# Four engines put in program order through branch A of a hybrid encoder block

## The chip, the cores and the metric

One core of one Trainium2 chip runs the whole block. The metric is the device time of one execution in microseconds. The engines are TensorE (PE, its weight loads PEld), VectorE (DVE), ScalarE (ACT), GpSimd (POOL) and SyncE (SP), which here issues nearly all DMAs.

## The reference, cut to what matters

1024 tokens and 16 meta tokens (1040 keys), width 1024. Branch A is differential attention with four heads: each has two attention maps, which are subtracted before they meet the values.

```python
s1 = einsum('bqhd,bkhd->bhqk', q1, k1) * scale - slope * dist
s2 = einsum('bqhd,bkhd->bhqk', q2, k2) * scale - slope * dist
attn = softmax(s1) - lam * softmax(s2)
y = rms_norm(einsum('bhqk,bkhe->bqhe', attn, v), subln_g) * (1 - lambda_init)
...
merged = sigmoid(ga) * (y_a @ w_ba) + sigmoid(gb) * (y_b @ w_bb)
```

The gates `ga` and `gb` are two projections of the normed input, 1024 columns each. A windowed attention (branch B) comes before the stretch that the change touches; the output projection and a SwiGLU feed-forward come after it.

## The kernel before

All matmuls keep float32 precision by splitting each operand into a high part (a copy that rounds, on ScalarE) and a low part (a subtraction, on GpSimd or VectorE), and adding three products.

**The loop over tiles.** The 32 tiles of branch A are four heads of eight query blocks (`n = 8 h + t`). A tile's work is written as generators, and the string `SLOTS = "sgsgsngsgsstntnt"` says in which order their steps are taken. TensorE runs in that order (`tc.manual_schedule`); where no such order is given, a planner that simulates the program orders an engine's instructions.

- `s`, six steps (`scores_a`): three chunks of 392, 392 and 256 keys for map 1, then three for map 0. TensorE makes the scores in a bank tagged `sc` (five of them); VectorE adds the distance and keeps a running minimum (line 817), writing to SBUF. With the minimum of the third chunk ScalarE takes the exponential of all 1040 columns and their sum (824); then VectorE takes the reciprocal (826), and for map 1 GpSimd scales by it and by minus lambda (828). At the end VectorE joins the maps: map 0 times its reciprocal plus map 1 (837) and a copy of the last 16 columns (838).
- `t`, three steps (`transpose_a`), for the tile before: TensorE transposes four, four and one blocks of 128 keys (849); ScalarE writes the high part (852), VectorE the low part (853).
- `n`, three steps of the tail: after every second tile the values (862), in three parts; after every fourth their norm: square and scaled copy on ScalarE (869, 871), sums on TensorE, a factor on VectorE and GpSimd (877, 878), the product on VectorE (884), a store.
- `g`, four steps (six in tile 1): one quarter each of a gate's matmuls (751), twelve of 512 columns a gate. Four steps go ahead of head 0 and ten ahead of each other head. So head 0 has 38 steps and a head of eight tiles 42: head 1 starts in the middle of gate 9, head 2 with gate 20, head 3 in the middle of gate 30. After the ten steps a gate starts at a tile's first `g` in heads 1 and 3, and at its third in head 2, as in head 0 from tile 2 on.

**The gates.** 50 partial products (`order_g`), seven for each of eight blocks but those made earlier. Gates 0 to 17 have kinds 2, 5 and 3; from gate 18 on two each of 1, 6, 7 and 4 take turns. For each, a raw weight is loaded (624; five buffers, asked for four gates ahead) and split into `gop` (117 and 118, four buffers, three gates ahead). A result of kind 1, 6 or 7 is added by VectorE to a sum kept from earlier (756), which is loaded from DRAM into one of three buffers `gk` when the weight is split (636); other results are copied by ScalarE (759, two buffers). Then it is stored (760). Two consecutive products use one bank of TensorE's results after another, two banks in all.

**Head changes.** At the top of a head's first tile the loads of its queries, keys and values are asked for (671 to 688). Their tiles have one buffer each, so a load waits for its last reader in the head before.

**Held back.** In tile 0 alone ScalarE and VectorE run in program order; there the splits are put into a list `held_back`, and `let_go` takes them out one at a time.

Of the kernel before, what the change touches and what calls it, by code (L numbers as in the profile page):

```python
# [19 lines left out]
P = 128  # L20
# [7 lines left out]
AH = 4  # L28
# [8 lines left out]
N_WAIT = 3  # L37
PP2 = 2
# [35 lines left out]
def encoder_block(ctx: ExitStack, tc: tile.TileContext, x, meta, norm_mix, w_in, lq1, lk1, lq2, lk2,  # L74
# [553 lines left out]
    def g_split(n, op=None):  # L628
        p, k = order_g[n]
        if op is None:  # L630
            op = gpool.tile([P, 2, 4, P], F32R, tag="gop", name=f"gop{p}_{k}", bufs=GO_BUFS)
        split(op[:, 0], op[:, 1], g_raw.pop((p, k)), nc.gpsimd)
        g_ready[p, k] = op
        if p in (1, 6, 7):
            kept = g_kept[p, k] = gpool.tile([P, 512], F32, tag="gk", name=f"gk{p}_{k}", bufs=GK_BUFS)
            nc.sync.dma_start(kept, g_place(p, k))
# [38 lines left out]
    def load_a0(h, q, k):  # L675
        q[0] = apool.tile([P, S], F32R, tag="q0", name=f"aq{h}_0")
        nc.sync.dma_start(f32(q[0]), qa_d[h][0])
        if h:
            load_k(h, 0, k[0])
            return q, k, load_v(h)  # L680
        return q, k
# [59 lines left out]

    def gate_steps():
        for n, (p, k) in enumerate(order_g):
            g_ahead(n + 1)
            op, act = g_ready.pop((p, k)), G_ACT[p]
            if p in (2, 5, 1):
                g_bank[k] = pp_bank(f"pg{p}_{k}")
            ps = g_bank[k]
            for c in range(4):
                for i, (a, b) in enumerate(((0, 0), (0, 1), (1, 0))):  # L750
                    nc.tensor.matmul(ps, op[:, a, c], quad(b, *act)[:, c], start=(p in (2, 5, 1) and c == 0 and i == 0),  # L751
                                     stop=(p in (2, 3, 4) and c == 3 and i == 2), skip_group_check=True)
                if c == 3:
                    if p in (1, 6, 7):
                        st = g_kept.pop((p, k))
                        nc.vector.tensor_tensor(st, ps, st, ALU.add)  # L756
                    else:
                        st = gpool.tile([P, 512], F32, tag="g", name="gate_stage", bufs=G_BUFS)
                        nc.scalar.copy(st, ps)
                    nc.sync.dma_start(g_place(p, k), st)  # L760
                    if (p, k) in ((5, 3), (5, 7), (3, 7)):
                        later_p = {(5, 3): 6, (5, 7): 7, (3, 7): 4}[p, k]
                        load_sums(later_p, *G_ACT[later_p])
                yield
# [9 lines left out]
    ld = *ld, load_v(0)  # L774
# [24 lines left out]
    behind_first, n_tile = [], [0]  # L799

    def scores_a(h, t, ld, s):
        slope = 2.0 ** -(2 * (h + 1))
        qs, ks, _ = ld
# [3 lines left out]
        u0 = 896 - t * P  # L807
        for m in (1, 0):
            s[m] = s0s[t % 2] if m == 0 else apool2.tile([P, L], F32, tag="s1", name=f"as1_{nm}", bufs=S_BUFS[1])
            low = far_a  # L810
            for i, (k0, n) in enumerate(A_CHUNKS):
# [8 lines left out]
                if i == 1 and behind_first:  # L820
                    behind_first.pop(0)()
                if i < 2:
                    yield
            nc.scalar.activation(s[m][:, 0:L], s[m][:, 0:L], AF.Exp, bias=low, scale=-1.0, accum_out=dn[:, m:m + 1])  # L824
            def scaled(m=m):
                nc.vector.reciprocal(dn[:, m:m + 1], dn[:, m:m + 1])  # L826
                if m:
                    (nc.gpsimd if t % 4 in COMBINE_POOL else nc.vector).tensor_scalar(  # L828
                        s[1][:, 0:L], s[1][:, 0:L], dn[:, 1:2], neglam, ALU.mult, ALU.mult)
            if m and n_tile[0] == 0:  # L830
                behind_first.append(scaled)
            else:
                scaled()
            if n_tile[0] == 0:
                let_go(1)
            yield
        nc.vector.scalar_tensor_tensor(s[0][:, 0:L], s[0][:, 0:L], dn[:, 0:1], s[1][:, 0:L], ALU.mult, ALU.add)
# [28 lines left out]
    def normed_a(h, c, py):  # L866
# [3 lines left out]
        yg = apool2.tile([P, 512], F32, tag="yg", name=f"yg_{nm}", bufs=2)  # L870
# [27 lines left out]
    def turn(done):  # L898
        h, t, s, at_, v = done
        yield from transpose_a(h, t, s[0], at_)  # L900

    def later(done):
        h, t, s, at_, v = done
        if t % 4 == 1:
            acc[0] = bank(psum2, "acc", f"apy_{h}_{t}", 1)
        yield from values_a(h, t, v, at_, acc[0])
# [10 lines left out]

    for n in range(AH * NT + T_LAG):
        n_tile[0] = n
        if n == 0:  # L920
            order_first = tc.manual_schedule(engines={mybir.EngineType.Activation, mybir.EngineType.DVE})
            order_first.__enter__()
        scoring, turning = iter(()), iter(())
        if n < AH * NT:
            h, t = divmod(n, NT)
            if t == 0:
                if h:
                    ld = load_a0(h, *load_a1(h))
# [3 lines left out]
            s = [None, None]  # L932
            tiles.append((h, t, s, at_, ld[2]))
# [5 lines left out]
        if n >= T_LAG:  # L939
            turning = turn(tiles[n - T_LAG])  # L940
        for what in SLOTS if n != 1 else "sgsgsngsgssggtntnt":
            if what == "s":
                next(scoring, None)
            elif what == "t":
                next(turning, None)
            elif what == "n":
                step_tail()
            else:
                fill(1)
        for _ in scoring:  # L950
            pass
        if n == 0:
            let_go(9)
            held_back = None
            order_first.__exit__(None, None, None)
# [3 lines left out]
        for _ in turning:  # L959
            pass  # L960
# [586 lines left out]
```

## Time and profile before

| | us |
|---|---|
| median of three runs | 1442.53 (1442.18 to 1443.05) |
| the profiled execution | 1443.88 |
| its span, first to last instruction | 1442.1 |
| granted TensorE clock | 0.998 |

A timeline line gives the start in us from the start of the span, the duration (of several merged instructions from the first's start to the last's end), engine, line, operation, what it writes from what it reads, shapes, the count, and in brackets the idle time before it with what ended it. A waits line reads: who, for whom, us in total, times, longest. A windows line gives the stretch, its length, the busy time and count of PE, PEld, DVE, ACT and POOL, the granted clock, the DMA engines' share and GB/s. In the chain of waits a piece has its start and its length. A DMA line ends with the size and the median time to landing. L817 is line 817.

### The profile page before, as it was taken

What the parts mean: (1) busy time and instruction counts of PE and PEld (TensorE: products, weight loads), DVE (VectorE), ACT (ScalarE), POOL (GpSimd) and SP (SyncE); (2) the same over time, 40 slices, a digit from 0 to 9 for tenths busy, and PEclk for the clock granted to TensorE, in tenths of its full rate; (3) what the DMA queues carried; (4) which work ended last, traced back from release to release, by engine and by line L of the source; (5) the groups of instructions that cost most, each with busy time, mean ns of one, the idle gap of its engine ahead of it and who ended that gap; (6) DMA issues with size and microseconds to landing.
All of it is one profiled execution on the core that took longest, in us unless ns stands there. A gap on an engine that the chain in (4) does not pass through costs nothing.

```text
span 1442.1 us, 21169 instructions
## 1 busy us (share of the span) xinstructions
PE 1421.4 (99%) x7279; PEld 1219.8 (85%) x7279; DVE 898.4 (62%) x1624; ACT 679.3 (47%) x1290; POOL 644.5 (45%) x605
## 2 busy tenths in 40 slices
PE   8999999999999999999999999999999999999997
PEld 6988989988889989888888788888888888788886
DVE  7468536637787979625514966555555554787567
ACT  6366535546565655545314643333333333444444
POOL 5589227744333433425522775544454442000444
PEclk9999999999999999999999999999999999999999
DMA  8367668996558464586602534333333333964443
GB/s 245 87 211 231 196 160 273 278 286 230 176 177 271 133 220 148 183 258 209 212 22 102 154 99 164 101 105 103 110 100 103 98 109 101 327 207 142 124 129 139
DMA packets 188891, 242.41 MB, mean 168 GB/s; under 512 B 18208, under 2 KB 115936, under 8 KB 188784
## 3 DMA queue, kind: packets, MB, share of 16 engines
q1 hardware_dynamic: 188784, 241.07, 52.9%
q8 instruction: 57, 0.93, 0.3%
q14 instruction: 50, 0.41, 0.1%
HBM read 157.45 MB, written 77.00 MB: 163 GB/s over the span
## 4 chain that ended last, share of the span: by engine, by line
PE 82%; POOL 6%; issue 4%; DVE 4%; DMA 3%; ACT 1%; SPq 0%; POOLq 0%; ACTq 0%; DVEq 0%
PE pg L1328 28%; PE pg L751 8%; PE pd L1422 8%; PE po L1105 6%; PE ppa L796 6%; PE aps L814 4%; PE apy L862 3%; PE pp_qb L214 3%; POOL oa L118 3%; PE pp_ka L214 2%; PE pp_va L214 2%; PE apt L849 2%; PE pp_qa L214 2%; PE bpt L356 1%; PE bpy L362 1%
## 5 line engine op out<-in xcount | busy, mean ns | idle before, releaser
L118 POOL TENSOR_TENSOR wop<-wf,wop 128x512 fp32r<-128x512 f32 x128 | 171.8, 1347 | 166.4 <-ACT wop L117 150.5
L1328 PE MATMUL pg<-t,wop 128*128 128x512 f32 x1056 | 242.6, 389 | 0.0
L1328 PEld LDWEIGHTS pg<-t,wop 128*128 128x128 f32 x1056 | 198.3, 188 | 41.1
L1422 PE MATMUL pd<-ob,oa 128*128 128x512 f32 x924 | 210.7, 390 | 0.8 <-POOL oa L118 0.4
L1422 PEld LDWEIGHTS pd<-ob,oa 128*128 128x128 f32 x924 | 173.2, 188 | 38.2 <-DVE ob L118 1.1
L1328 PE MATMUL pg<-b,wop 128*128 128x512 f32 x792 | 185.6, 392 | 2.4 <-DVE c L1337 2.4
L1328 PEld LDWEIGHTS pg<-b,wop 128*128 128x128 f32 x792 | 149.5, 189 | 34.2 <-issue 2.4
L751 PE MATMUL pg<-hT_hi,gop 128*128 128x512 f32 x384 | 142.3, 395 | 0.0
L118 POOL TENSOR_TENSOR oa<-ra,oa 128x512 fp32r<-128x512 f32 x33 | 44.0, 1336 | 171.2 <-ACT oa L117 169.8
L117 ACT ACTIVATE wop<-wf 128x512 fp32r<-128x512 f32 x128 | 80.2, 631 | 83.2 <-PE pg L1328 48.6
L118 POOL TENSOR_TENSOR gop<-gr,gop 128x512 fp32r<-128x512 f32 x47 | 66.0, 1406 | 106.3 <-ACT gop L117 106.3
L117 ACT ACTIVATE oa<-ra 128x512 fp32r<-128x512 f32 x77 | 48.7, 632 | 106.1 <-PE pd L1422 45.3
L824 ACT ACTIVATE as<-as,amn 128x1040 f32<-128x1040 f32 x64 | 74.5, 1164 | 45.4 <-DVE amn L817 34.4
L1163 DVE TENSOR_TENSOR s<-wf,wf 128x512 f32<-128x512 f32 x22 | 25.5, 1160 | 105.6 <-DMA wf<-in_w_ff_gate_dram 57.7
L814 PE MATMUL aps<-ak,aq 128*128 128x392 f32 (+1 forms) x384 | 89.3, 327 | 1.6 <-DVE amn L817 1.1
L1105 PE MATMUL po<-woh,mT 128*128 128x512 f32 x384 | 88.0, 390 | 0.0
L1105 PEld LDWEIGHTS po<-woh,mT 128*128 128x128 f32 x384 | 71.9, 188 | 14.8
L751 PEld LDWEIGHTS pg<-hT_hi,gop 128*128 128x128 f32 x384 | 72.2, 188 | 11.2 <-DVE gk L756 0.2
L814 PEld LDWEIGHTS aps<-ak,aq 128*128 128x128 f32 x384 | 69.3, 188 | 14.6 <-DVE amn L817 2.0
L343 POOL TENSOR_SCALAR bs<-bs,bdn 128x432 f32<-128x432 f32 (+1 forms) x64 | 41.4, 665 | 85.9 <-DVE bdn L341 74.1
L751 PE MATMUL pg<-hT_lo,gop 128*128 128x512 f32 x192 | 75.8, 395 | 0.0
L828 POOL TENSOR_SCALAR as<-as,adn,neglam 128x1040 f32<-128x1040 f32 x32 | 38.9, 1216 | 57.5 <-DVE adn L826 43.9
(289 smaller groups left out, 3099.4 us busy)
## 6 DMA issues: line engine op xcount, KB each, us to landing
ra<-aop SPq DMA_DIRECT2D x77, 256.0 KB, 2.7
wf<-in_w_ff_gate_dram SPq DMA_DIRECT2D x24, 512.0 KB, 3.9
wf<-in_w_ff_up_dram SPq DMA_DIRECT2D x24, 512.0 KB, 3.9
aop<-as SPq DMA_DIRECT2D x44, 256.0 KB, 2.1
w_c<-in_w_in_dram SPq DMA_DIRECT2D x17, 512.0 KB, 6.1
aop<-c SPq DMA_DIRECT2D x33, 256.0 KB, 2.0
ts_d<-to SPq DMA_DIRECT2D x16, 512.0 KB, 3.8
gw<-in_w_in_dram SPq DMA_DIRECT2D x32, 256.0 KB, 4.1
```

Source lines behind the costliest of these rows:

```text
L117: nc.scalar.activation(hi, src, AF.Copy)
L118: lo_eng.tensor_tensor(lo, src, f32(hi), ALU.subtract)
L214: nc.tensor.matmul(ps[:, :n], a[:, c, :], b[:, c, at:at + n], start=(c == 0 and i == 0), stop=(c == DC - 1 and i == 2))
L343: nc.gpsimd.tensor_scalar(st[:, r, :W], st[:, r, :W], dn[:, r:r + 1], 1.0, ALU.mult, ALU.mult)
L751: nc.tensor.matmul(ps, op[:, a, c], quad(b, *act)[:, c], start=(p in (2, 5, 1) and c == 0 and i == 0), stop=(p in (2, 3, 4) and c == 3 and ...
L796: nc.tensor.matmul(ps, w[:, a, j, :], src(j, b, tk), start=(j == 0 and n == 0), stop=(j == 3 and n == 2))
L814: nc.tensor.matmul(ps[:, :n], qs[m][:, t * P:(t + 1) * P], ks[m][:, vv, k0:k0 + n], start=(vv == 0), stop=(vv == 1))
L824: nc.scalar.activation(s[m][:, 0:L], s[m][:, 0:L], AF.Exp, bias=low, scale=-1.0, accum_out=dn[:, m:m + 1])
L862: nc.tensor.matmul(py[:, cols], v[:kp, a, k, :], at_[:kp, k, b, :], start=(k == 0 and j == 0), stop=(k == 8))
L1105: nc.tensor.matmul(ps, mT[:, c, a, t * P:(t + 1) * P], wos[q, c][:, b], start=(c == 0 and n == 0), stop=(c == DC - 1 and n == 2))
L1328: nc.tensor.matmul(ps, op[:, x, c, :], b[:, y, c, :], start=(p in (1, 2, 5) and c == 0 and n == 0), stop=(p in (4, 2, 3) and c == 3 and n ...
L1422: nc.tensor.matmul(ps[u], oa[:, a, u * P:(u + 1) * P], ob[:, b, :], start=(p in (1, 2, 5) and j == 0 and k == 0), stop=(p in (2, 3, 4) and ...
```

## The change

- A manual order for ScalarE, VectorE, GpSimd and SyncE (`order_av`) spans the whole loop of branch A; before, ScalarE's and VectorE's covered tile 0 alone.
- `scores_a` only makes scores. The exponential (`exp_a`), the scaling of map 1 (`scale_a`) and the join (`join_a`) are called from the loop: exponential 1 after the third `s`, scaling after the fifth, exponential 0 after the first `t` (`EXP_AT`), the join of the tile before after the first `s` (`JOIN_AT`).
- A gate's result is written down one step later (`owed`, `gate_result`), behind the next gate's first quarter. With it goes the load of token sums into `hT`.
- Splits are held back through the whole loop; one is let go behind exponential 1 and one at the third `t`, or where a gate needs it at once.
- The load of a kept sum is put in a list with the split, and asked for after the second quarter of a gate, if fewer than three are held.
- The next head's loads are called in the last tile of a head: map 1's after the third `s`, map 0's after the sixth. Its values are loaded at tile 2.
- The scaled values `yg` have one buffer instead of two.

```diff
         if p in (1, 6, 7):
-            kept = g_kept[p, k] = gpool.tile([P, 512], F32, tag="gk", name=f"gk{p}_{k}", bufs=GK_BUFS)
-            nc.sync.dma_start(kept, g_place(p, k))
+            kept_to_do.append((p, k))
+
+    def load_kept():
+        p, k = kept_to_do.pop(0)
+        kept = g_kept[p, k] = gpool.tile([P, 512], F32, tag="gk", name=f"gk{p}_{k}", bufs=GK_BUFS)
+        nc.sync.dma_start(kept, g_place(p, k))
...
+    def gate_result(p, k, ps):
+        if p in (1, 6, 7):
+            while (p, k) not in g_kept:
+                load_kept()
+            st = g_kept.pop((p, k))
+            nc.vector.tensor_tensor(st, ps, st, ALU.add)
+        else:
+            st = gpool.tile([P, 512], F32, tag="g", name="gate_stage", bufs=G_BUFS)
+            nc.scalar.copy(st, ps)
+        nc.sync.dma_start(g_place(p, k), st)
...
     def gate_steps():
         for n, (p, k) in enumerate(order_g):
             g_ahead(n + 1)
+            while (p, k) not in g_ready:
+                let_go(1)
...
+                while owed:
+                    gate_result(*owed.pop(0))
+                if c == 1:
+                    while kept_to_do and len(g_kept) < GK_BUFS:
+                        load_kept()
                 if c == 3:
...
+                    owed.append((p, k, ps))
+                    if n == len(order_g) - 1:
+                        gate_result(*owed.pop(0))
...
+    def exp_a(s, m):
+        dn = s["of"]
+        nc.scalar.activation(s[m][:, 0:L], s[m][:, 0:L], AF.Exp, bias=s["low", m], scale=-1.0, accum_out=dn[:, m:m + 1])
+
+    def scale_a(t, s):
+        dn = s["of"]
+        nc.vector.reciprocal(dn[:, 1:2], dn[:, 1:2])
+        (nc.gpsimd if t % 4 in COMBINE_POOL else nc.vector).tensor_scalar(
+            s[1][:, 0:L], s[1][:, 0:L], dn[:, 1:2], neglam, ALU.mult, ALU.mult)
+
+    def join_a(s):
+        dn = s["of"]
+        nc.vector.reciprocal(dn[:, 0:1], dn[:, 0:1])
         nc.vector.scalar_tensor_tensor(s[0][:, 0:L], s[0][:, 0:L], dn[:, 0:1], s[1][:, 0:L], ALU.mult, ALU.add)
...
+    order_av = tc.manual_schedule(engines={mybir.EngineType.Activation, mybir.EngineType.DVE, mybir.EngineType.Pool, mybir.EngineType.SP})
+    order_av.__enter__()
     for n in range(AH * NT + T_LAG):
...
+        if n < AH * NT and t == 2 and h:
+            vs[h] = load_v(h)
+        scored = turned = 0
+        if n == AH * NT:
+            join_a(tiles[n - 1][2])
         for what in SLOTS if n != 1 else "sgsgsngsgssggtntnt":
...
+            if what == "s" and n < AH * NT:
+                next(scoring)
+                scored += 1
+                if scored == JOIN_AT and n:
+                    join_a(tiles[n - 1][2])
+                if scored == 3:
+                    exp_a(s, 1)
+                    if t == NT - 1 and h < AH - 1:
+                        ahead = load_a1(h + 1)
+                    let_go(1)
+                if scored == 5:
+                    scale_a(t, s)
+                if scored == 6 and n == 0:
+                    exp_a(s, 0)
+                if scored == 6 and t == NT - 1 and h < AH - 1:
+                    ahead = load_a0(h + 1, *ahead)
+            elif what == "t" and n:
+                next(turning)
+                turned += 1
+                if turned == EXP_AT and n < AH * NT:
+                    exp_a(s, 0)
+                if turned == 3:
+                    let_go(1)
...
+    order_av.__exit__(None, None, None)
     n_gates[0] += HOLD
     raw_w = []
     while tail:
         step_tail()
+        let_go(9)
         fill(3)
```

More of the change, by code (lines that the diff above doesn't have):

```diff
@@ L819, in scores_a @@
                 low = mn[:, m, i:i + 1]
-                if i == 1 and behind_first:
-                    behind_first.pop(0)()
                 if i < 2:
                     yield
[L824 to L835, printed above, removed]
-            yield
+            s["low", m] = low
+            yield
+    def exp_a(s, m):
[9 more added lines that the diff above has]
+        nc.vector.reciprocal(dn[:, 0:1], dn[:, 0:1])
         nc.vector.scalar_tensor_tensor(s[0][:, 0:L], s[0][:, 0:L], dn[:, 0:1], s[1][:, 0:L], ALU.mult, ALU.add)
@@ L927, in encoder_block @@
                 if h:
[L928 removed]
+                    ld = ahead
                 fill(G_HEAD if h else G_FIRST)
```

54 lines of the change are left out of this document (17 added, 37 removed).

## The prediction, made before the changed kernel was run

> **What bounds the kernel now.** I read the page's busy times first, then the busy time of the stretch that holds branch A's attention loop, then who waits there.
>
> ```profile
> PE 1421.4 (99%) x7279; PEld 1219.8 (85%) x7279; DVE 898.4 (62%) x1624; ACT 679.3 (47%) x1290; POOL 644.5 (45%) x605
> ...
> 325.00:605.00 280.00, 276.67 (x1699) 250.16 (x1697) 224.08 (x647) 167.55 (x316) 110.81 (x88) 1.00 0.59 193
> ...
> PE apt L849 <- DVE as L837: 1.1, 2, 1.0
> PE aps L814 <- DVE amn L817: 1.1, 3, 0.4
> PE aps L814 <- DMA ak<-ka_d: 0.5, 1, 0.5
> ```
>
> In these 280 us TensorE is busy 276.67 and idle 3.3; VectorE is busy 224, 80%. So TensorE bounds the loop, and all that a better order of the other engines can give back there is a few us: 1.1 waiting for the softmax difference, 1.1 for a score bank, 0.5 for a key load. What VectorE itself waits for costs TensorE almost nothing today.
>
> The tile is the unit to count in. The first score matmuls of five successive tiles (head 3, tiles 2 to 6) in the timeline:
>
> ```profile
> 542.51 0.60 PE L814 MATMUL aps<-ak,aq 128*128 128x392 f32 x2
> ...
> 549.07 0.63 PE L814 MATMUL aps<-ak,aq 128*128 128x392 f32 x2
> ...
> 556.26 0.61 PE L814 MATMUL aps<-ak,aq 128*128 128x392 f32 x2
> ...
> 563.83 0.60 PE L814 MATMUL aps<-ak,aq 128*128 128x392 f32 x2
> ...
> 572.48 0.60 PE L814 MATMUL aps<-ak,aq 128*128 128x392 f32 x2
> ```
>
> Tiles 2, 3, 4 and 5 take 6.56, 7.19, 7.57 and 8.65 us, 29.97 for a cycle of four, 7.49 a tile. TensorE's order is not changed. So what decides is whether the other engines, in the order now written down, can still do a tile in 7.49 us.
>
> **The written order, followed round once.** ScalarE and VectorE each run their list in order, so one late entry holds all behind it. From the new loop, tile n: the third score chunk of map 1, then its exponential (exp 1) on ScalarE; at the first transpose step ScalarE's high part of transpose block 0 of tile n-1, and only then exp 0 of tile n; at the next step block 1's high part on ScalarE and its low part on VectorE; then block 2. VectorE's next entry is the first score chunk of tile n+1, then the join of tile n (reciprocal, sum of the two maps, copy of 32 columns), then chunks 2 and 3, and then exp 1 of tile n+1. That closes a loop through both engines: exp 1, high 0, exp 0, high 1, low 1, low 2, chunk 1, reciprocal, sum, copy, chunk 2, chunk 3, exp 1. No link can be passed on its engine. Prices, from starts of instructions that follow each other without a gap in the timeline of VectorE and that of ScalarE:
>
> ```profile
> 544.20 0.61 DVE L817 CUSTOM_DVE_ANT_0 as<-aps,dist,far_a 128x392 f32<-128x392 f32 x1
> 544.75 0.68 DVE L853 TENSOR_TENSOR at<-apt,at 128x512 fp32r<-128x512 f32 x1
> 545.35 0.17 DVE L838 COPY as<-as 128x32 f32<-128x32 f32 x1
> 545.43 0.27 DVE L853 TENSOR_TENSOR at<-apt,at 16x128 fp32r<-16x128 f32 x1
> 545.63 0.60 DVE L817 CUSTOM_DVE_ANT_0 as<-aps,dist,amn 128x392 f32<-128x392 f32 x1
> ...
> 546.74 0.48 DVE L817 CUSTOM_DVE_ANT_0 as<-aps,dist_m,amn 128x256 f32<-128x256 f32 x1
> 547.15 0.69 DVE L756 TENSOR_TENSOR gk<-pg,gk 128x512 f32<-128x512 f32 x1
> 547.75 0.62 DVE L817 CUSTOM_DVE_ANT_0 as<-aps,dist,amn 128x392 f32<-128x392 f32 x1
> ...
> 550.38 0.16 DVE L826 RECIPROCAL adn<-adn 128x1 f32<-128x1 f32 x1
> 550.64 1.30 DVE L837 SCALAR_TENSOR_TENSOR as<-as,adn,as 128x1040 f32<-128x1040 f32 x1
> 551.86 0.62 DVE L817 CUSTOM_DVE_ANT_0 as<-aps,dist,amn 128x392 f32<-128x392 f32 x1
> ```
>
> ```profile
> 542.85 0.59 ACT L869 ACTIVATE ysq<-apy 128x512 f32<-128x512 f32 x1
> 543.33 0.69 ACT L871 ACTIVATE yg<-apy,gsub 128x512 f32<-128x512 f32 x1
> 543.90 0.28 ACT L852 ACTIVATE at<-apt 128x128 fp32r<-128x128 f32 x1
> ...
> 546.94 0.63 ACT L117 ACTIVATE gop<-gr 128x512 fp32r<-128x512 f32 x1 [2.76 <-issue]
> 547.48 1.15 ACT L824 ACTIVATE as<-as,amn 128x1040 f32<-128x1040 f32 x1
> 548.62 0.58 ACT L852 ACTIVATE at<-apt 128x512 fp32r<-128x512 f32 x1
> 549.10 1.16 ACT L824 ACTIVATE as<-as,amn 128x1040 f32<-128x1040 f32 x1
> 550.25 0.75 ACT L852 ACTIVATE at<-apt 128x512 fp32r<-128x512 f32 x2
> ```
>
> ScalarE: exp 1.14 (547.48 to 548.62), high 0 0.48, exp 0 1.15, high 1 0.58 until its result is there: 3.35. VectorE: low 1 0.60, low 2 0.20, chunk 1 0.55, reciprocal 0.26, sum 1.22, copy 0.08, chunk 2 0.55, chunk 3 0.48: 3.94. **The bare loop is 7.29 us.** Before, the same timeline shows the reciprocal and the sum starting at 550.38, while exp 0 (549.10) has only just ended, and blocks 1 and 2 after them: low 1, low 2 and chunk 1 were not between exp 0 and the sum. That is 1.35 us, and its loss is the heart of the change.
>
> On the loop come, by head:
> - the split of a gate weight, let go right behind exp 1: its copy stands between exp 1 and high 0, 0.54 (546.94 to 547.48). In heads 1 and 3, where a gate starts at a tile's first gate step, this is every tile; in heads 0 and 2 a gate starts at the third step, behind the place where splits are let go, and the split falls to the last transpose step, off the loop.
> - the gate result. In heads 1 and 3 it is written behind the join: its ScalarE copy is off the loop, its addition on VectorE is on it, 0.60 (547.15 to 547.75). In heads 0 and 2 it is written behind exp 1: the ScalarE copy is on the loop, 0.48, taken from the row below; an addition makes exp 0 wait for the last chunk of map 0: 0.60 + 0.55 + 0.55 + 0.16 + 0.48 = 2.34 on VectorE against 1.62 on ScalarE, so 0.72.
> - the square and the scaled copy of four tiles' values, once in four tiles, in the step behind exp 1: 0.48 + 0.57 = 1.05.
>
> Cycles of four: head 0 (copies) 4 x 7.77 + 1.05 = 32.1. Head 1 (splits) 4 x 7.83 + 1.05 = 32.4. Head 2 (three additions in four, one copy: 0.66 on average) 4 x 7.95 + 1.05 = 32.9. Head 3 (splits, additions three times in four) 4 x 8.28 + 1.05 = 34.2. Against 29.97 that is 2.1, 2.4, 2.9 and 4.2 a cycle; two cycles a head: **23.2 us.** This takes it that TensorE's long tile (8.65) lets the loop catch up what the short one (6.56) lost. Where it can't, each tile costs the longer of the two: in head 1 8.65 + 8.88 + 7.83 + 7.83 = 33.2, 3.2 a cycle, and likewise 3.0, 3.6 and 4.6 in heads 0, 2 and 3: 28.8 in all. From below: at a head's start TensorE has ten gate steps alone, and what lag is left then is hidden.
>
> ```profile
> 451.43 6.95 PE pg L751 x30
> ...
> 472.10 1.07 PE apy L862 x9
> ```
>
> (The second line, nine value matmuls, is for the next part.) Of the 6.95 us at most the lead that the five score banks allow is used: five chunks of at most 0.60 by the rows above and a gate step of 6.95 / 10 = 0.7 between them, 3.7 us a head: 23.2 - 14.8 = 8. I take 23, the sum itself: the lag cannot grow beyond the banks, so it is nearly as long in a head's second tile as in its last, and what a fill hides at its end is built up anew.
>
> **The splits held back all through.** At the start of gate n the split of gate n+3 is only queued; two places a tile let one go. The ten steps at a head's start queue two or three and let none go. In heads 1 and 3 they are let go in time. Head 2 begins with gate 20, so gate 23 starts at the third gate step of its first tile, one step behind the place that lets its split go. VectorE starts on that tile's chunk 1 0.4 us in, and ends chunk 3 0.55 + 0.26 + 1.22 + 0.08 + 0.55 + 0.48 = 3.1 later; then exp 1, the copy, and GpSimd:
>
> ```profile
> 547.65 1.28 POOL L118 TENSOR_TENSOR gop<-gr,gop 128x512 fp32r<-128x512 f32 x1 [4.32 <-ACT gop L117]
> ```
>
> High part ready at 0.4 + 3.1 + 1.14 + 0.63 = 5.3, low part at 6.6. TensorE is there after three chunks (at most 0.6 each), two steps of 0.7 and nine value matmuls (1.07): 4.3 or sooner; its third matmul, which takes the low part, 0.46 later. It waits 1.0 or more, then some 0.9: I take 2.5 us, once (0 if VectorE is far ahead, 3.3 if the chunks take half).
>
> **SyncE in order.** The load of a kept gate sum goes into one of three buffers, the next of which is just being stored; everything behind it on SyncE's queue stands. Behind it in a head's last tile stand the next head's eight query and key loads.
>
> ```profile
> SPq L636 <- DMA g_d<-gk: 30.0, 19, 3.9
> ...
> 446.43 0.33 SPq L671 DMA_DIRECT2D aq<-qa_d  x1
> ...
> 450.98 0.46 SPq L666 DMA_DIRECT2D ak<-ka_d  x1
> ...
> ak<-ka_d SPq DMA_DIRECT2D x12, 260.0 KB, 8.0
> ```
>
> Before, a kept load waited up to 3.9. For head 2 the loads went out from 446.43 to 450.98, so the last landed about 459.0; its first scores start after the fill, at 458.4, and map 0 is wanted some 4 us later. A delay of 3.9 makes map 0 late by about 0.5. Heads 2 and 3 can be hit. At head 1 the stores of gate results queue behind the head's loads:
>
> ```profile
> 395.16 0.59 ACT L759 COPY gate_stage<-pg 128x512 f32<-128x512 f32 x1 [5.21 <-DMA g_d<-gate_stage]
> 395.64 1.17 ACT L824 ACTIVATE as<-as,amn 128x1040 f32<-128x1040 f32 x1
> ```
>
> ScalarE stood 5.21 there and an exponential behind it. The new order keeps both buffers and the same neighbours, so it stays and may reach the next tile. I put +3 for the three head starts: from -2 (the value load, 1 MB, moved out of their way to tile 2, where values are first used late in tile 3) to +4 at each, +12. The store asked for one step later, the second buffer less for the scaled values (next used four tiles on) and the earlier order of loads cost nothing beside that. The waits of before that were quoted, 2.7, may go: -1 (0 to -3.3).
>
> **Sum.** 23 + 2.5 + 3 - 1 = +27.5. The profiled execution took 1443.88 us with a span of 1442.1, 1.3 above the median of 1442.53; the same addition to the median gives **1470**.
>
> [...] Sums and copies of VectorE are sometimes stretched:
>
> ```profile
> 514.42 1.30 POOL L118 TENSOR_TENSOR gop<-gr,gop 128x512 fp32r<-128x512 f32 x1 [0.74 <-ACT gop L117]
> ...
> 514.59 2.24 DVE L837 SCALAR_TENSOR_TENSOR as<-as,adn,as 128x1040 f32<-128x1040 f32 x1
> ```
>
> The sum took 2.24 instead of 1.30, and started 0.17 into a subtraction of GpSimd that ended 1.13 later: 1.13 + 1.22 = 2.35, so it waited it out. [...]
>
> **Rivals.**
> - *GpSimd under the join.* In heads 0 and 2 the split let go at the last transpose step puts GpSimd's 1.28 us where the join begins, on the loop: behind exp 0 come high 1, high 2 and the copy, 0.48 + 0.28 + 0.63 = 1.4, so GpSimd works from 1.4 to 2.7, and the sum is due at 0.58 + 0.60 + 0.20 + 0.55 + 0.26 = 2.2. That is 0.5 a tile, 0.94 at worst (2.24 less 1.30), over 16 tiles: +8 to +15, 1478 to 1485. Against: a weight that is late shifts GpSimd past the sum.
> - *SyncE decides.* +12 instead of +3 at the head starts and gate weights late behind them: 1480 to 1486. Against: weights are asked for four gates ahead.
> - *The lag is carried.* TensorE's lead and the fills take half of it or more: +8 to +19, 1450 to 1462.
> - *Faster.* The loop stays under 7.49, because the splits and gate results that stand on it fall into time in which ScalarE or VectorE would wait for the other anyway; then TensorE keeps its pace, the join comes always in time, and the 3.3 us of idle time in the stretch go: 1439. It decides at 29.97 a cycle, which the bare loop (4 x 7.29 + 1.05 = 30.2) only just misses. Against: the entries named stand between two links of the same engine, where there is no such time.
> - *Nothing:* the planner's order was already this one, and the time stays at 1442.5. Against: the rows from 549 to 552 stand in another order.
>
> **How the numbers follow.** Forecast 0.60 (its own range 1462 to 1480), carried lag 0.13, GpSimd 0.09, SyncE 0.05, faster 0.09, nothing 0.04. The range goes from the bottom of the carried lag, 1450, to near the top, 1484; faster, nothing and a part of the top, under 0.2, are left out. About 0.2% (2.9 us) is what can be told from no change. Slower 0.60 + 0.13 + 0.09 + 0.05 = 0.87, same 0.04, faster 0.09.
>
> **What would show it.** In the changed profile: tiles 2 and 3 of a cycle near 8 to 9 us instead of 6.56 and 7.19; ScalarE idle 3 to 4 us a tile before exp 1, put down to the third chunk's minimum; VectorE in the order low 1, low 2, chunk 1, sum; TensorE waiting before transposes for the sum and before score chunks for a bank; about 2.5 us before gate 23. After 620 us nothing but a shift. It is wrong if tiles keep their 6.56, or if TensorE's waits are for loads and not for VectorE.

## The result, and the profile after

The changed kernel took 1495.32 us (median of four runs, 1493.36 to 1499.97) beside 1442.79 for the kernel before: a ratio of 1.037, with an interval of 1.034 to 1.039. That is 52.5 us slower. The forecast was 27.5 slower, with 41.5 as the top of its range. Direction and place were right, the size was not.

The first part of the page after, then the stretches of the four heads (a windows view), then TensorE's waits from 320 to 660 us. The changed kernel has other line numbers: 836 makes the scores, 839 is VectorE's chunk, 849 the exponential, 860 the sum of the maps, 872 the transposes, 875 and 876 the high and low parts, 892 and 894 the square and the scaled copy, 898 the sums of squares, 119 and 120 the split of a weight, 776 the gate's matmuls, 756 and 759 their results.

```profile
PE 1446.1 (97%) x7279; PEld 1236.6 (83%) x7279; DVE 906.0 (61%) x1624; ACT 674.1 (45%) x1290; POOL 638.7 (43%) x605
```

```profile
326.00:401.00 75.00, 67.71 (x366) 58.38 (x365) 51.22 (x148) 39.32 (x76) 24.93 (x20) 0.95 0.43 134
401.00:483.00 82.00, 73.61 (x419) 65.23 (x418) 56.67 (x160) 39.91 (x78) 24.68 (x21) 0.94 0.57 184
483.00:566.00 83.00, 72.92 (x417) 64.87 (x416) 59.13 (x164) 38.07 (x73) 26.02 (x22) 0.94 0.49 158
566.00:640.00 74.00, 66.80 (x389) 60.92 (x388) 55.83 (x159) 35.70 (x69) 22.96 (x20) 0.91 0.38 125
```

```profile
PE apst L898 <- ACT ysq L892: 15.3, 7, 2.3
PE apt L872 <- DVE amn L839: 9.5, 12, 1.3
PE pg L776 <- ACT gop L119: 2.7, 2, 2.4
PE pg L776 <- POOL gop L120: 1.6, 3, 0.6
PE aps L836 <- DVE amn L839: 1.3, 3, 0.5
PE aps L836 <- DMA ak<-ka_d: 1.2, 1, 1.2
```

No engine has more instructions than before. TensorE, idle for 3.3 of 280 us in the loop before, now stands 33 us in these 314 (314 less the four busy times, 281.0), and its granted clock is 0.91 to 0.95 where it was 1.00. The longest wait is not one that the prediction priced for TensorE: the sums of squares (`apst`) wait seven times for ScalarE's square, 2.2 us each on average (1.81 to 2.33). Next come the transposes that wait for the softmax; loads are 1.2.

What the other engines wait for turned as foreseen. ScalarE before its exponentials and VectorE before its low parts, from the groups of the page after, and the same two groups of the loop before:

```profile
L849 ACT ACTIVATE as<-as,amn 128x1040 f32<-128x1040 f32 x64 | 74.5, 1164 | 133.4 <-DVE amn L839 133.3
...
L876 DVE TENSOR_TENSOR at<-apt,at 128x512 fp32r<-128x512 f32 (+1 forms) x96 | 50.1, 550 | 49.0 <-ACT at L875 48.9
```

```profile
L824 ACT ACTIVATE as<-as,amn 128x1040 f32<-128x1040 f32 x64 | 74.5, 1164 | 45.4 <-DVE amn L817 34.4 <-DVE as L838 8.9 <-POOL gop L118 1.4
```

```profile
L853 DVE TENSOR_TENSOR at<-apt,at 128x512 fp32r<-128x512 f32 (+1 forms) x96 | 50.8, 547 | 7.9 <-ACT at L852 7.7
```

ScalarE's idle time before an exponential that the minimum ends went from 34.4 to 133.3 us, and VectorE's for ScalarE's high part from 7.7 to 48.9. Each of the two stands for the other, while neither has more to do: that is the loop.

The tiles of head 3 after, by their first score matmuls, to be laid beside 6.56, 7.19, 7.57 and 8.65:

```profile
582.67 0.60 PE L836 MATMUL aps<-ak,aq 128*128 128x392 f32 x2
...
594.07 1.00 PE L836 MATMUL aps<-ak,aq 128*128 128x392 f32 x2
...
602.80 0.61 PE L836 MATMUL aps<-ak,aq 128*128 128x392 f32 x2
...
610.37 0.60 PE L836 MATMUL aps<-ak,aq 128*128 128x392 f32 x2
...
619.86 0.60 PE L836 MATMUL aps<-ak,aq 128*128 128x392 f32 x2
```

Tiles 2 to 5 take 11.40, 8.73, 7.57 and 9.49. The same reading of every tile, summed by place over the heads, with the loss against the same tiles before:

| tiles | before (heads 0, 1, 2, 3) | after | loss |
|---|---|---|---|
| 0 and 1 of heads 1 to 3 | 18.05, 16.09, 16.13 | 20.42, 21.03, 16.13 | +7.3 |
| 2 | 6.19, 6.53, 6.51, 6.56 | 8.93, 10.52, 11.62, 11.40 | +16.7 |
| 3, 4 and 5 | 23.98, 23.65, 23.36, 23.42 | 26.92, 24.25, 25.00, 25.79 | +7.6 |
| 6 | 6.51, 6.53, 6.78, 6.53 | 10.47, 10.74, 10.72, 11.72 | +17.3 |
| 7 of heads 0 to 2 | 14.69, 14.40, 15.42 | 16.45, 16.24, 15.15 | +3.3 |

These are 52.2; the last tile and its tail add 1.8, and everything after the loop is 2.4 shorter. Two thirds (34.0) lie in tiles 2 and 6, and seven of those eight are the tiles in which the square of four tiles' values stands. The eighth, tile 2 of head 0, has no values before it and takes 8.93.

**What a tile with a square looks like.** The timelines of TensorE, ScalarE and VectorE in head 1:

```profile
426.65 0.66 PE L872 MATMUL apt<-ident,as 128*128 128x128 f32 x4 [0.44 <-DVE amn L839]
429.64 1.34 PE L898 MATMUL apst<-ones,ysq 128*128 128x1 f32 x8 [2.33 <-ACT ysq L892]
430.84 1.31 PE L872 MATMUL apt<-ident,as 128*128 128x128 f32 x5
431.80 1.00 PE L836 MATMUL aps<-ak,aq 128*128 128x392 f32 x2
```

```profile
427.33 1.16 ACT L849 ACTIVATE as<-as,amn 128x1040 f32<-128x1040 f32 x1 [3.49 <-DVE amn L839]
...
428.49 0.61 ACT L119 ACTIVATE gop<-gr 128x512 fp32r<-128x512 f32 x1
429.01 0.58 ACT L892 ACTIVATE ysq<-apy 128x512 f32<-128x512 f32 x1
429.49 0.68 ACT L894 ACTIVATE yg<-apy,gsub 128x512 f32<-128x512 f32 x1
430.06 0.59 ACT L875 ACTIVATE at<-apt 128x512 fp32r<-128x512 f32 x1
430.53 1.18 ACT L849 ACTIVATE as<-as,amn 128x1040 f32<-128x1040 f32 x1
...
431.97 0.77 ACT L875 ACTIVATE at<-apt 128x512 fp32r<-128x512 f32 x2 [0.17 <-PE apt L872]
...
436.99 1.16 ACT L849 ACTIVATE as<-as,amn 128x1040 f32<-128x1040 f32 x1 [3.77 <-DVE amn L839]
```

```profile
432.60 0.88 DVE L876 TENSOR_TENSOR at<-apt,at 128x512 fp32r<-128x512 f32 x2 [1.16 <-ACT at L875]
433.41 0.60 DVE L839 CUSTOM_DVE_ANT_0 as<-aps,dist,far_a 128x392 f32<-128x392 f32 x1
...
434.20 1.30 DVE L860 SCALAR_TENSOR_TENSOR as<-as,adn,as 128x1040 f32<-128x1040 f32 x1
...
435.63 0.62 DVE L839 CUSTOM_DVE_ANT_0 as<-aps,dist,amn 128x392 f32<-128x392 f32 x1
...
436.40 0.48 DVE L839 CUSTOM_DVE_ANT_0 as<-aps,dist_m,amn 128x256 f32<-128x256 f32 x1
```

Exp 1, split, square, scaled copy, high 0, exp 0, high 1 and 2, low parts, chunk 1, sum, chunk 2, chunk 3: the predicted loop, once round from 427.33 to 436.99. TensorE has done its first four transposes and comes to the sums of squares; the square stands behind exp 1 and the split, so TensorE stops for 2.33 us in the middle of a tile. Its last five transposes stand behind those sums and are done at 432.15, so ScalarE's next copy (0.17) and VectorE's low parts behind it (1.16) wait as well. In such a tile the loop runs through TensorE too.

**What a tile without one looks like.** The next exponentials of map 1, in tiles 4 and 5 of head 1:

```profile
445.30 1.17 ACT L849 ACTIVATE as<-as,amn 128x1040 f32<-128x1040 f32 x1 [3.78 <-DVE amn L839]
...
453.60 1.17 ACT L849 ACTIVATE as<-as,amn 128x1040 f32<-128x1040 f32 x1 [3.77 <-DVE amn L839]
```

From 436.99 to 445.30 and from there to 453.60 the loop goes round in 8.31 us, and to the next, at 461.91, in 8.31 again, while TensorE's own lengths of these tiles were 7.43, 7.58 and 8.64 before. The loop runs at a pace of its own. Such plain rounds take, from tile 3 on, 8.50 in head 0, 8.31 in head 1, 8.53 to 8.89 in head 2 and 8.91 in head 3.

The same trace's granted clock, the third number from the end of a windows row: two 3.4 us stretches that hold such a stop, and in a second answer of the same view what followed each.

```profile
426.80:430.20 3.40, 1.07 (x9) 0.83 (x9) 2.23 (x9) 2.87 (x6) 0.96 (x1) 1.00 0.71 225
461.00:464.40 3.40, 0.84 (x6) 0.60 (x6) 2.46 (x11) 2.49 (x5) 0.64 (x1) 1.00 1.01 326
```

```profile
430.20:433.60 3.40, 3.40 (x15) 3.21 (x15) 1.76 (x5) 2.84 (x6) 2.51 (x3) 0.51 0.02 7
464.40:471.20 6.80, 6.80 (x25) 6.22 (x25) 4.33 (x10) 2.73 (x6) 2.84 (x3) 0.50 0.50 190
```

TensorE was busy for 1.07 and 0.84 of 3.40 us, and was then granted half its clock for 3.4 and 6.8 us. The trace has seven such pairs in the loop, one for each wait for a square, 41 us at half clock in all; before, the loop had none.

### The profile page after: what moved, and what is told of

Read it like the earlier page. It is cut to its first block, busy times and chain, and to the rows that moved or that the text cites. A ratio compares the mean times of both kernels' runs of the same rounds, so it can differ in the third digit from the quotient of the medians.

```text
span 1494.1 us, 21147 instructions
## 1 busy us (share of the span) xinstructions
PE 1446.1 (97%) x7279; PEld 1236.6 (83%) x7279; DVE 906.0 (61%) x1624; ACT 674.1 (45%) x1290; POOL 638.7 (43%) x605
## 4 chain that ended last, share of the span: by engine, by line
PE 70%; DVE 7%; POOL 7%; ACT 6%; issue 6%; DMA 4%; SPq 0%; POOLq 0%; DVEq 0%; ACTq 0%
PE pg L1367 26%; PE pd L1461 8%; PE ppa L819 6%; PE po L1144 5%; PE pg L776 5%; PE pp_qb L216 3%; POOL oa L120 3%; PE pp_va L216 2%; DVE as L839 2%; ACT as L849 2%; PE pp_ka L216 2%; PE pp_qa L216 2%; DVE as L860 2%; PE aps L836 2%; PE bpt L358 1%
## 5 line engine op out<-in xcount | busy, mean ns | idle before, releaser
L120 POOL TENSOR_TENSOR wop<-wf,wop 128x512 fp32r<-128x512 f32 x128 | 171.8, 1346 | 165.3 <-ACT wop L119 151.5
L776 PE MATMUL pg<-hT_hi,gop 128*128 128x512 f32 x384 | 148.0, 409 | 5.2 <-ACT gop L119 2.7
L120 POOL TENSOR_TENSOR gop<-gr,gop 128x512 fp32r<-128x512 f32 x47 | 60.6, 1290 | 176.2 <-ACT gop L119 142.8
L849 ACT ACTIVATE as<-as,amn 128x1040 f32<-128x1040 f32 x64 | 74.5, 1164 | 133.4 <-DVE amn L839 133.3
L836 PE MATMUL aps<-ak,aq 128*128 128x392 f32 (+1 forms) x384 | 94.4, 342 | 2.9 <-DVE amn L839 1.3
L776 PEld LDWEIGHTS pg<-hT_hi,gop 128*128 128x128 f32 x384 | 75.8, 197 | 19.4 <-ACT gop L119 3.2
L836 PEld LDWEIGHTS aps<-ak,aq 128*128 128x128 f32 x384 | 73.1, 199 | 17.1 <-DVE amn L839 1.9
L1144 PEld LDWEIGHTS po<-woh,mT 128*128 128x128 f32 x384 | 71.9, 188 | 14.8
L876 DVE TENSOR_TENSOR at<-apt,at 128x512 fp32r<-128x512 f32 (+1 forms) x96 | 50.1, 550 | 49.0 <-ACT at L875 48.9
```

Of the source, the lines that this page charges most:

```text
L120: lo_eng.tensor_tensor(lo, src, f32(hi), ALU.subtract)
L836: nc.tensor.matmul(ps[:, :n], qs[m][:, t * P:(t + 1) * P], ks[m][:, vv, k0:k0 + n], start=(vv == 0), stop=(vv == 1))
L876: nc.vector.tensor_tensor(lo, pt[:lo.shape[0], :nb], f32(hi)[:lo.shape[0]], ALU.subtract)
L1144: nc.tensor.matmul(ps, mT[:, c, a, t * P:(t + 1) * P], wos[q, c][:, b], start=(c == 0 and n == 0), stop=(c == DC - 1 and n == 2))
```

## The experiments

Most are one run each, beside one run of the kernel before; those stood between 1443.4 and 1447.4, so a difference of two single runs is good to about 5 us. The text below goes by the length of the loop alone, which leaves out what varies elsewhere: in each trace, from branch A's first score matmul to the first matmul of its projection: 292.8 us before, 346.7 after. The table gives it as a difference to before; it too comes from one trace each.

| run | time, us | beside it | loop |
|---|---|---|---|
| after | 1495.32 | 1442.79 | +54.0 |
| e1: all edits, no hand order | 1445.92 | 1447.36 | +3.0 |
| e2: ScalarE, VectorE by hand | 1501.79 | 1444.25 | +58.2 |
| e3: GpSimd, SyncE by hand | 1457.47 | 1447.36 | +15.0 |
| e4: four by hand, join and exp 0 at 3 | 1461.02 | 1447.36 | +17.8 |
| e7: exp 0 at 3 alone | 1489.95 | 1443.37 | +47.0 |
| e8: join at 3 alone | 1480.30 | 1443.37 | +37.2 |
| e6: TensorE kept busy | 1491.04 | 1447.36 | +49.5 |
| e9: square ahead of exp 1 | 1484.58 | 1444.25 | +41.3 |
| e10: e2 with e4 and e9 | 1453.77 | 1444.25 | +10.4 |
| e13: e10, a split let go in the fill | 1448.66 | 1443.37 | +5.2 |
| e11: e3, two kept sums | 1451.21 | 1444.25 | +8.6 |
| e14b: all remedies, four by hand | 1458.17 | 1444.74 | +14.9 |
| e15: e13, kept sums asked for early | 1452.95 | 1444.74 | +9.2 |

Measured against the expectations below, e1, e4 and e13 came out in the range of the first case named, e7, e10 and e14b in that of the second; e2, e3, e6, e8, e9, e11 and e15 fell in neither.

**Which part of the change costs the time?** The hand order was taken away altogether (e1), and given to two engines at a time (e2, e3).

```diff
-    order_av = tc.manual_schedule(engines={mybir.EngineType.Activation, mybir.EngineType.DVE, mybir.EngineType.Pool, mybir.EngineType.SP})
-    order_av.__enter__()
...
-    order_av.__exit__(None, None, None)
```

> All edits of the change stand, but no order by hand on ScalarE, VectorE, GpSimd and SyncE in branch A: the planner orders them. Theory A (the order by hand closes a loop between ScalarE and VectorE, and the idle time it makes takes TensorE's clock down): 1440 to 1450, no half clock between 320 and 680 us. Rival B (the late kept sums, late values and held-back splits cost it, whoever orders them): over 1470.

```diff
-    order_av = tc.manual_schedule(engines={mybir.EngineType.Activation, mybir.EngineType.DVE, mybir.EngineType.Pool, mybir.EngineType.SP})
+    order_av = tc.manual_schedule(engines={mybir.EngineType.Activation, mybir.EngineType.DVE})
```

> The order by hand only on ScalarE and VectorE; the planner orders GpSimd and SyncE. If the loop through ScalarE and VectorE and SyncE's waits are two costs that add, it takes the changed kernel's time less the 10 us of the run with GpSimd and SyncE alone: 1480 to 1487. If SyncE's order is needed for the loop to cost so much: under 1470.

(e3 names Pool and SP there instead.)

> The order by hand only on GpSimd and SyncE; the planner orders ScalarE and VectorE. Theory A: 1442 to 1455, square waits (TensorE for the square of the values) under 3 us in total instead of 15.3. Rival C (SyncE's order, kept loads behind stores, decides): over 1475, with TensorE waiting for loads or gate weights.

All other edits together, with the planner's order, can't be told from the kernel before by their time (1445.92 beside 1447.36); the loop in that trace is 3.0 longer. The orders are what costs. ScalarE and VectorE alone lose more (+58.2) than all four, with 5.1 and 5.0 us of TensorE's waits for a gate weight and a gate's result where the changed kernel has 2.7 and 1.0; GpSimd and SyncE alone lose +15.0. The parts do not add. Most of e3's loss is at head 2, whose first two tiles take 25.3 us instead of 16.1. SyncE's queue there, then VectorE in the same trace:

```profile
461.41 0.32 SPq L760 DMA_DIRECT2D g_d<-gk  x1
470.01 0.32 SPq L644 DMA_DIRECT2D gk<-g_d  x1
```

```profile
472.74 0.69 DVE L756 TENSOR_TENSOR gk<-pg,gk 128x512 f32<-128x512 f32 x1 [7.41 <-DMA gk<-g_d]
```

The load of a kept sum (the second row) started 8.28 us after the end of the first row, which stores its buffer. VectorE's addition then waited 7.41 us for that sum, with score chunks behind it. ScalarE stood longer, 12.08 us until 469.45, for a gate weight; that one was asked for at 460.27, before the store, so its lateness is not the kept sum's doing. The wait for the buffer was foreseen, its length was taken as 3.9.

**Is it the loop through ScalarE and VectorE?** Two constants move the join behind the third score chunk and exp 0 behind the last transpose step, which opens the loop: both (e4), and one each (e7, e8).

```diff
-JOIN_AT = 1
-EXP_AT = 1
+JOIN_AT = 3
+EXP_AT = 3
```

> All four engines by hand, but exponential 0 after the third transpose step and the join after the third score step (EXP_AT = 3, JOIN_AT = 3): low 1, low 2 and chunk 1 leave the way from exponential 0 to the join. Theory A: the loop is shorter, 1450 to 1465, and the tiles that follow a value pair drop from 10.5 us to under 8. Rival C: no change worth naming, 1490 or more.

> The changed kernel with exponential 0 after the third transpose step alone (EXP_AT = 3, JOIN_AT = 1). It takes low 1 and low 2 (0.80 us) and the high parts behind exponential 0 from the way between exponential 0 and the join. The two positions together gave -34 us. If the high and low parts behind exponential 0 are the dear link: 1465 to 1475. If the join ahead of chunks 2 and 3 is: 1485 or more.

> The changed kernel with the join after the third score step alone (EXP_AT = 1, JOIN_AT = 3): exponential 1 no longer waits for the reciprocal, the sum and the copy (1.56 us) and, in heads 1 and 3, for the gate's addition. If the join ahead of chunks 2 and 3 is the dear link: 1462 to 1472. If it is the high and low parts behind exponential 0: 1485 or more.

Both take 36.2 of the 54.0 away; join alone 16.7, exp 0 alone 7.0. Opened at one link, the loop closes through the other: in e8 exp 1 still comes round every 8.30 us in head 1, and the longest of TensorE's waits becomes

```profile
PE apt L872 <- DVE as L860: 20.7, 23, 1.5
```

many short ones for the sum, now late. With both moved, head 1's tiles 2 to 5 are 6.94, 7.64, 7.57 and 8.64: TensorE's own pace, within 0.4 of before. That settles the loop, and that it takes both links. With both moved TensorE's wait for the square is 0.4 us instead of 15.3, though nothing was done to the square: it was late because the loop made exp 1 late.

**What are the square and the clock worth?** In e6 ten matmuls whose results are thrown away fill the bank ahead of the sums of squares, so that TensorE works where it would stand. In e9 the square and the scaled copy are written down at the end of the tile before, ahead of exp 1.

```diff
         pst = bank(psum2, "sc", f"apst_{nm}", SC)
+        for _ in range(10):
+            nc.tensor.matmul(pst, hT_hi[:, 0, 0:P], hT_hi[:, 0, 0:512], start=True, stop=True)
```

> The changed kernel with ten matmuls of 512 columns whose result is thrown away (2.3 us) just ahead of the sums of squares, eight times: TensorE works where it stood idle for the square. Clock theory: the half-clock stretches in branch A shrink or vanish and the time falls to 1475 to 1485, though TensorE does more. Rival (the clock costs nothing, the waits are all): 1495 or up to 10 us more.

```diff
+        if n > 1 and n % 4 == 1:
+            h_, t_, _, _ = tiles[n - 2]
+            square_a(h_, t_ // 4, acc[0])
```

> The changed kernel, but ScalarE's square and scaled copy of four tiles' values are written at the end of the tile before, so they run ahead of exponential 1 and not behind it. If the wait of TensorE for the square (15.3 us) and the half clock that follows it are the part that the prediction lacked: the tiles that held the sums of squares go from 10.5 to 11.7 us down to 8 to 9, the half-clock stretches mostly go, and the time is 1465 to 1478. Rival (the bare loop of exponentials, low parts and join makes nearly all of it): 1487 or more.

With TensorE kept busy the half clock in the loop falls from 41 to 10 us, the wait for the square is gone from its list, and 4.5 us are won: the clock's part, as far as one can take it alone (the eighth set of thrown-away matmuls fills no such wait and costs some itself: the last tile takes 43.20 instead of 41.58). Half of 41 would be 20 (the half-clocked pair of score matmuls at 594.07 takes 1.00 us, the other four 0.60 or 0.61), so most of the half-clocked time seems, by this estimate, to have fallen where TensorE would have stood for the loop anyway. With the square out of the way 12.7 us are won, and 20 us at half clock are left. Tiles 2 and 6 of e9 take 8.0 to 9.2, above the 7.8 to 8.3 that the prediction gave the loop without a square, and tiles 2 to 7 still lose 31.3 of their 44.9 us. The longest of TensorE's waits there is

```profile
PE apt L872 <- DVE amn L839: 12.8, 17, 1.3
```

**What is left of each pair?** ScalarE and VectorE by hand with both remedies (e10: the diffs of e4 and e9 on e2), then with one split let go in each head's fill (e13); GpSimd and SyncE with two kept sums ahead instead of three (e11).

> ScalarE and VectorE by hand with both links undone (exponential 0 after the third transpose step, the join after the third score step, the square early), GpSimd and SyncE by the planner. Theory A: nothing of the loop is left above a tile's TensorE time, 1438 to 1446, as before or a few us better. Rival (any order by hand on these two costs 10 us or more): 1453 or more.

```diff
                     ld = ahead
+                if h:
+                    let_go(1)
```

> As the run with ScalarE and VectorE by hand, both links undone and the square early (1453.8), and one held-back split let go right behind the ten gate steps of a head's start. If the late split of gate 23 makes head 2's first tile 13.2 us long: that tile falls to 8 to 10, 1447 to 1451. Rival (a gate weight that lands late from DRAM, behind the head's loads): 1453 or more.

```diff
-                    while kept_to_do and len(g_kept) < GK_BUFS:
+                    while kept_to_do and len(g_kept) < GK_BUFS - 1:
```

> GpSimd and SyncE by hand as in the run before, but at most two kept gate sums held, so that a kept load goes into a buffer stored a whole gate ago and does not wait for the store just asked for. If that wait (SyncE stood from 461.7 to 470.0 us behind a store queued after the head's loads, and gate weights came late) makes the 10 us: 1446 to 1450, head 2's first two tiles near 7.5 and 8.7 instead of 12.7. Rival (the splits held back through the whole loop, or the loads' new places): 1454 or more.

e2's +58.2 falls to +10.4 and +5.2, e3's +15.0 to +8.6. In e13 tiles 2 to 5 of head 1 stand at 6.82, 7.36, 7.57 and 8.64, and TensorE no longer waits for a gate weight. One tile is left long, head 2's first, 10.62 instead of 7.46, where VectorE has

```profile
460.30 0.69 DVE L756 TENSOR_TENSOR gk<-pg,gk 128x512 f32<-128x512 f32 x1 [5.49 <-DMA gk<-g_d]
```

an addition that waits for its kept sum, with the score chunks behind it. In e11 the first two tiles of head 2 are back to 16.6; the rest is spread over head 0's tiles 1 and 2 (16.5 instead of 13.2), head 1's first (11.0 instead of 9.4) and others, and was not traced to its cause.

**Do the remedies add?** All of them under all four hand orders: e14, and the same kernel again as e14b.

> All found so far, with all four engines by hand: exponential 0 and join at three, the square early, two kept sums at most, one split let go at a head's start. If the parts add: 1442 to 1450. If SyncE by hand still holds the head starts up: 1455 or more.

> All four engines by hand, with the four remedies together: join and exponential 0 after the third step, square and scaled copy ahead of exp 1, two kept sums instead of three, one split let go in each head's fill. If the parts are the whole of the loss and add up: what is left of ScalarE and VectorE by hand (+5.3) and of GpSimd and SyncE by hand (+7.0), less the kept-sum wait of 5.5 us at head 2 that the first of them still has: 1448 to 1455. If the hand orders meet in a wait that neither pair shows alone: over 1458. Granted clock 0.99 or more, as in the runs with the pairs.

e14 took 6784 us. Its trace, by stretches:

```profile
0.00:300.00 300.00, 292.36 (x1794) 264.88 (x1795) 181.25 (x372) 158.77 (x355) 180.16 (x233) 1.00 0.72 211
300.00:1000.00 700.00, 700.00 (x751) 555.09 (x751) 95.58 (x263) 81.62 (x148) 53.11 (x54) 0.17 0.12 40
```

From about 300 us on TensorE was granted 0.17 of its clock, through stages that no edit touches, and the same kernel then ran in 1458.17 with 0.995. That execution says nothing of the kernel, and its cause is open. e14b's ratio is 1.009 (1.007 to 1.011). Its +14.9 in the loop is near the 5.2 and 8.6 of the two pairs together, but that is partly luck, for the tiles do not add: tiles 1 and 2 of head 0 lose 0.7 us where e11 loses 3.4, and head 2's first tile (14.50 us) loses 7.0 where e13 loses 3.2 and e11 0.5. VectorE's wait list from 450 to 480 us leads with

```profile
DVE gk L756 <- DMA gk<-g_d: 10.7, 1, 10.7
```

a wait for a kept sum that is 5.5 at most in e13 and 1.8 in e11: the hand orders meet in a wait that neither pair shows at this length.

**Can the kept sum come earlier?** e15 asks for it when its weight is split, as before the change.

```diff
             kept_to_do.append((p, k))
+            load_kept()
```

> ScalarE and VectorE by hand with the three remedies, GpSimd and SyncE left to the planner, and a kept sum asked for when its weight is split, as before the change. If the 5.3 us that this version still lost came from VectorE standing 5.49 us for a kept sum in head 2's first tile, that tile drops from 10.62 to about 7.5 to 8 and the time to 1444 to 1446. If a kept sum comes no earlier because its buffer is not free, the time stays at 1447 to 1450.

It does not help: ratio 1.005 (1.003 to 1.007), and head 2's first two tiles are 12.2 and 11.1 long, with 9.0 us of VectorE still spent waiting for two kept sums. In SyncE's queue the load of the second went out at 464.14, 3.23 us after the end of the entry before it in the queue, the store of a sum (460.91); VectorE had that sum at 468.90, after 4.69 us of waiting. No version run here is measurably faster than the kernel before.

## Why the prediction was off

**Bound and mechanism: right.** TensorE's order and work are unchanged, and the written loop decides. The rows show its entries in the predicted order, ScalarE idle before exp 1 for 3.4 to 4.9 us in nearly all tiles (3 to 4 were foreseen), and nothing but a shift after the loop; e4 opens the loop and takes two thirds of the loss away. TensorE's longest waits are for VectorE and ScalarE, not for loads.

**The step that failed: the terms of the sum over "cycles of four", 23 us.** Tiles 2 to 7 lost 44.9. Tile 3 came within the 8 to 9 us that were to show the step right in heads 1 to 3 (8.03, 8.67, 8.73); tile 2 did so only in head 0, where it has no square (8.93). Both terms of the sum were too small, the round of the loop and the square. e9 tells them apart, as far as one trace can: with the square out of the way tiles 2 to 7 lose 31.3, where the sum without its 8.4 for squares had 14.8. So about 16.5 of the 21.7 us that the sum lacked are the plain round's, and 5.2 the square's.

- *The round: 7.77, 7.83, 7.95 and 8.28 us in heads 0 to 3.* It takes 8.50, 8.31, 8.53 to 8.89, and 8.91: about 15 us more over the 23 tiles, an estimate from these numbers. In head 1 the rows from 434.20 to 436.99 show where. From the sum to chunk 2 (434.20 to 435.63) it is 1.43, priced as 1.30; from chunk 2 to chunk 3 (to 436.40) 0.77, priced as 0.55; from chunk 3 to exp 1 (to 436.99) 0.59, priced as 0.48. That makes 0.46 of the 0.48. The prices came from rows in which the next entry doesn't use the result of the one before, and for the last from a bare duration; in the loop the copy uses the sum, chunk 3 the minimum of chunk 2, exp 1 that of chunk 3. Chunk 3 starts 0.77 or 0.78 after chunk 2 in 30 of the 32 tiles.
- *The square as 1.05 us "on the loop".* It was priced as two entries on ScalarE's list. But TensorE also stands for it in mid-tile, with five transposes queued behind its sums, and these hold the loop up once more. A tile with a square in head 1 was to take 8.88 (7.83 + 1.05) and took 10.52 and 10.74; in head 3, 9.33 against 11.40 and 11.72. e9 puts the square's place at 12.7 us in the whole loop where the sum had 8.4.
- *No term for the granted clock.* 41 us at half clock came with those stops. e6 gives them 4.5 net. They are part of the square's 12.7, but how large a part stays open, since e9 keeps 20 us of half clock.

*"TensorE's long tile lets the loop catch up what the short one lost"* held: exp 1 comes every 8.31 us through tiles 3, 4 and 5 of head 1, whether TensorE's own tile is shorter or longer. With the measured plain rounds (8.8 on average in head 2) and its own 1.05 for a square the same sum gives about 45 us. That this meets the 44.9 is partly luck, for the squares cost more, and the 44.9 leave out the first two tiles of each head and the last. The lower bound, a lag hidden in the fills, and the rival built on it pointed the wrong way.

**Head starts: right within the change, but covered.** The 2.5 us for gate 23's split came as 2.42 and 0.62 us of waiting in head 2's first tile; +3 for SyncE and this together make 5.5 against 7.3 measured in the first two tiles of heads 1 to 3. Taken alone the term was too small: GpSimd and SyncE by hand cost 15.0 in the loop (e3) and about 10 in time, close to the +12 that the rival of a deciding SyncE was given. In the changed kernel part of that seems hidden, since a late gate delays what is late already: with the loop open, in e4, the first two tiles of heads 1 to 3 lose 11.2 instead of 7.3.

**The other rivals.** *GpSimd under the join* came, at under half its price of 0.5 us: in heads 0 and 2 most sums start with 0.41 to 0.45 us of a split's subtraction on GpSimd still to run, end 1.10 after it and so take 1.51 to 1.54 us; in tiles 2 to 7 of heads 1 and 3, with none beside them, they take 1.30. That is some 0.2 of what the round of heads 0 and 2 has too much. Over all tiles the sums average 1423 ns where they took 1346,

```profile
L860 DVE SCALAR_TENSOR_TENSOR as<-as,adn,as 128x1040 f32<-128x1040 f32 x32 | 45.5, 1423 | 3.4
```

2.5 us over 32 tiles, for before three were stretched too, to 1.51, 1.74 and 2.24, each ending 1.10 after such a subtraction. *Faster* and *lag carried* fell with the tile lengths; *nothing* fell with ScalarE's wait lists.

## What to carry to other kernels

When an order is written by hand, follow the dependence once round through all engines, TensorE among them: an entry that TensorE needs in mid-tile (here a square, waited for 1.81 to 2.33 us) costs its whole lateness there, not its own length on the list (here 1.05 with the scaled copy). Price each link from a row in which the next entry uses the result of the one before; rows that merely follow each other made this round 0.46 us too short, and it is paid in every tile. Afterwards read the round itself, from one entry to the same entry a tile later: it tells the loop's pace, which the bottleneck's tile lengths blur. Here seven stops of 1.81 to 2.33 us in a busy TensorE also came with half the clock for 3.4 or 6.8 us each, so read the granted clock wherever a new wait appears.

## What the runs showed of the hardware

In the changed kernel all seven drops of the granted clock in the loop began at the end of a 3.4 us stretch in which TensorE was busy for 0.66 to 1.20 us, a fifth to a third of it, and lasted 3.4 or 6.8 us; no stop in the loop was longer than 2.42 us. The busy share of such a stretch gives no clean limit: from 486.0 to 489.4 TensorE was busy for 0.98 of 3.4 us, with the stop of 2.42 in it (for a gate weight), and the clock stayed at 1.00. Nor does the length of a single wait: in e8, with waits of up to 1.7 us and TensorE idle for 31.1 of 314 us, the four heads' stretches all show 1.00; in e9, with 24.5 idle and one wait of 2.4 but no other above 1.4, they show 0.95 to 0.98. One execution (e14) ran at 0.16 to 0.17 of the clock from about 300 us on, read up to 6700 of its 6782 us. And VectorE's chunk of 392 with a running minimum was followed by the next chunk, which starts from that minimum, 0.77 us after its start (435.63 to 436.40), but by an entry that doesn't use it 0.55 after (544.20 to 544.75 before the change).
